# Memory's norm taken from the transposed copy of memory, and the first transfers cut in halves, in a two-layer decoder trunk

## The chip, the cores and the metric

The kernel runs on one core of one Trainium2 chip. The metric is the device time of the core in microseconds (us); a smaller number is better. Engines: TensorE (PE; its weight loads are listed as PEld), VectorE (DVE), ScalarE (ACT), GpSimd (POOL) and SyncE (SP), whose queue issues most of the DMA transfers.

## What is computed

A trunk of two layers over x (512 x 1024) with a memory of 256 rows of 1024. Each layer normalises x, projects it, runs 12 heads of forgetting attention (layer 0) or retention (layer 1) and 4 heads of attention over the memory, gates the result and projects it back:

```python
def reference(x, mem, norm_g, ...):
    mem_n = rmsnorm(mem, mem_norm_g)
    for i in range(DEPTH):
        h = rmsnorm(x, norm_g[i])
        ...
        memo = mem_cross_attention(q_mem, mem_n, w_mem_kv[i])
        o = jnp.concatenate([main, memo], axis=-1) * jax.nn.silu(z)
        x = x + o @ w_out[i]
    return rmsnorm(x, final_norm_g)

def rmsnorm(x, g):
    y = xf * lax.rsqrt(jnp.mean(xf * xf, axis=-1, keepdims=True) + EPS)
    return (y * g.astype(jnp.float32)).astype(x.dtype)

def mem_cross_attention(q_mem, mem_n, w_kv):
    kv = mem_n @ w_kv
    km, vm = split_cols(kv, [MEM_W, MEM_W])
    ...
```

The change is about `mem_n @ w_kv`. The kernel multiplies the unnormalised memory (times the gains) with the weights and applies the reciprocal root mean square of each memory row afterwards.

## The kernel before, in words

All weights come from DRAM in pieces of 128 x 1024 fp32 (512 KB). `load_piece` (L110) issues the transfer of the next piece of a fixed list on SP's queue into one of four buffers `raw`. `prep_piece` (L122) splits it in two rounded parts: a cast to `wH` on ScalarE (L136) and the remainder `wL = raw - wH` on VectorE (L137), each in one of four buffers; it then issues the next load. A piece is split when an earlier one is retired by TensorE. Only the first piece's cast is shared by VectorE (L131) and ScalarE (L132). Each product is computed as three: high x high, high x low, low x high.

The program starts with memory. `start_mem` (L743) issues, on SP's queue, the transposed memory in two halves of 512 KB (`vv<-in_memT_dram`; each holds four of the eight slices of 128 columns), four weight pieces, a small table, and then memory's 256 rows as they are, two transfers of 512 KB. The gains `gc` are a small transfer on ScalarE's queue. Then `emit` (L896) fills a warm-up tile with zeros on VectorE (L900) and runs 13 products of it on TensorE (L904). `first_splits` and `mem_split` split memory's slices, times the gains, in two parts (tiles `gg`; L768 and L160 on ScalarE, L769 and L161 on VectorE).

Real work begins with the values of layer 1 (`f_vm(1, ...)`): four pieces, in each two slices of memory against 512 columns, for two blocks of 128 memory rows: 12 products of 512 columns a piece, 48 in all, into two accumulators. The first piece's products stand with all `wH` first (L437), the others' mixed (L450). Four key heads follow (`f_km(1, h)`), 24 products of 256 columns each (L60). Then layer 0's keys and values of memory and the rest.

`memr_gen` (L774) makes the reciprocal roots: two squares over memory's rows with a running sum on ScalarE (L175), two small steps on GpSimd (L176, L177) for each of the two. The result `mr` scales the values as they leave PSUM, and `spread` (L180) turns it into a row over all partitions, `rbm`, by two products with the unit matrix (L183) and a copy (L185); the keys are multiplied by `rbm` (L417).

TensorE's order is the order in which the program is written (`MANUAL`). While the first four pieces are split, VectorE, ScalarE and GpSimd are also in written order. Elsewhere a scheduler places their instructions by priorities (`due`), and so the order on these engines shows in the built program only. SP is in written order up to the first layer.

Of the kernel before, what the change touches and what calls it, by code (L numbers as in the profile page):

```python
# [16 lines left out]
D = 1024  # L17
# [18 lines left out]
@with_exitstack  # L36
def tile_hybrid(ctx, tc, x_in, mem_in, memT_in, g_cols, norm_g, fin_g, b_f, wv0, wp, index, consts, cosT, sinT, dec, out):
    nc = tc.nc
# [41 lines left out]
    rbm = cst.tile([P, NMEM], F32, name="rbm")  # L80
    ident = csb[:, 0:P]
    nhalf = cst.tile([P, 1], F32, name="nhalf")
    G.memset(nhalf, -0.5)
# [84 lines left out]
    def acc_tile():  # L168
        return ps_at("acc", [P, 512], F32, name="acc")
# [233 lines left out]
    def f_km(l, h):  # L403
        key = (l, "km", h)

        def fn():
            H, L = pieces[key]
            mT = st["mT"]
            ps = acc_tile()
            terms = []  # L410
            for w, c in ((H, 0), (H, 1), (L, 0)):
                for k in range(KD):
                    terms.append((w[:, k * P:(k + 1) * P], mT[k][c]))
            mm_group(ps[:, :NMEM], terms)
            kt = tile_("km" if l == 0 else "qk", [P, 2, NMEM], F32R)
            kn = tile_("dd", [P, 512])
            V.tensor_tensor(out=kn[:, :NMEM], in0=ps[:, :NMEM], in1=rbm, op=ALU.mult)  # L417
            split_to(kt[:, 0, :], kt[:, 1, :], kn[:, :NMEM])
            st[l, "km", h] = kt
            retire(key)  # L420
        return [([key], fn)]

    def f_vm(l, plan, first=False):
        box = {}
        seen = {}

        def part(steps, final):
            mT = st["mT"]
            if first and steps[0][0] == 0:
                H, L = pieces[l, "vm", 0]  # L430
                for _, b in steps:
                    box[b] = acc_tile()
                for w, halves in ((H, (0, 1)), (L, (0,))):
                    for _, b in steps:
                        for k2 in range(2):
                            for c in halves:
                                PE.matmul(box[b], lhsT=mT[k2][c][:, b * P:(b + 1) * P], rhs=w[:, k2 * 512:(k2 + 1) * 512],  # L437
                                          start=(w is H and k2 == 0 and c == 0), stop=False)
                retire((l, "vm", 0))
                steps = []  # L440
            for i, b in steps:
                H, L = pieces[l, "vm", i]
                if b not in box:
                    box[b] = acc_tile()
                n = 0
                for k2 in range(2):
                    k = 2 * i + k2
                    for a, w in split3(mT[k][0][:, b * P:(b + 1) * P], mT[k][1][:, b * P:(b + 1) * P],
                                       H[:, k2 * 512:(k2 + 1) * 512], L[:, k2 * 512:(k2 + 1) * 512]):
                        PE.matmul(box[b], lhsT=a, rhs=w, start=(i == 0 and n == 0), stop=(i == 3 and n == 5))  # L450
                        n += 1
                seen[i] = seen.get(i, 0) + 1
                if seen[i] == 2:
                    retire((l, "vm", i))
            if final:
                if l == 1:
                    vm = [t[:, :1024].rearrange("p (b c) -> p b c", b=2) for t in pt_tiles()]
                else:
                    vm = [tile_("vv", [P, 2, 512], F32R) for _ in range(2)]
                for b in range(2):  # L460
                    split_to(vm[0][:, b, :], vm[1][:, b, :], box[b], st["mr"][b])
                st[l, "vm"] = vm
# [214 lines left out]
    def g_forget():  # L677
# [45 lines left out]
        norm=(0, 2),  # L723
        memr=(0, 2.4),
        xload=(0, 1, 2, 3, 4),
# [17 lines left out]
    def start_mem():  # L743
        nc.scalar.dma_start(out=gc, in_=g_cols)
        src = [tile_("vv", [P, 4, NMEM]) for _ in range(2)]
        rows = [tile_("vv", [P, D]) for _ in range(2)]
        nc.sync.dma_start(out=src[0], in_=memT_in[0])
        load_piece()
        nc.sync.dma_start(out=src[1], in_=memT_in[1])
        for _ in range(BUFS["raw"] - 1):  # L750
            load_piece()
        nc.sync.dma_start(out=csb, in_=consts[:, 0:P])
        for b in range(2):
            nc.sync.dma_start(out=rows[b], in_=mem_in[b * P:(b + 1) * P, :])
        st["msrc"], st["mrows"] = src, rows
# [29 lines left out]
    def build_layer(l):  # L785
# [13 lines left out]
        for pr in range(6):  # L799
# [28 lines left out]
    cycle(f_vm(1, [[(i, 0), (i, 1)] for i in range(4)], first=True) +  # L828
          sum([f_km(1, h) for h in range(4)], []), [("memr", (), 1.5), ("xload", (), 0.5)], mode=8)
    cycle(sum([f_km(0, h) for h in range(4)], []) + f_vm(0, [[(i, 0), (i, 1)] for i in range(4)]),  # L830
# [64 lines left out]
    def emit():  # L895
# [18 lines left out]
        for ci, (fillers, jobs, start, mode, last) in enumerate(cycles):  # L914
            if start == ("lead", 0):
                spill()
                lead.close()
                tro = tile_("dd", [P, 2 * P])
                tc.keep_in_program_order(nc.sync.dma_start(out=tro, in_=consts[:, P:3 * P]))
                tc.keep_in_program_order(A.copy(out=tri, in_=tro[:, :P]))  # L920
                tc.keep_in_program_order(A.copy(out=ones, in_=tro[:, P:]))
                nc.sync.dma_start(out=bfb, in_=b_f.partition_broadcast(P))
# [43 lines left out]
    tri = cst.tile([P, P], F32R, name="tri")  # L966
    ones = cst.tile([P, P], F32R, name="ones")
    bfb = cst.tile([P, 12], F32, name="bfb")
# [100 lines left out]
```

## Time and profile before

| what | value |
|---|---|
| median of 3 runs | 925.57 us (925.4 to 925.78) |
| the profiled execution | 925.52 us, its span 923.7 us |
| TensorE busy | 914.7 us of the span |
| VectorE, ScalarE, GpSimd busy | 593.5, 437.2, 33.6 us |
| DMA moved | 100.69 MB |

The span runs from the first to the last instruction. A row of the timeline gives the start, the busy time, the engine, the line, the operation and its tiles; in brackets stands how long the engine had been idle before, and what ended that. A busy engine is not an engine that could do no more: VectorE and ScalarE have room, and their idle time costs nothing while TensorE has its next operands in time.

### The profile page before, as it was taken

Reading aid. Unit: us, or ns where it says so; the run is one execution under the profiler, and the core shown is the slowest. Engines: PE = TensorE matmul, PEld = TensorE weight load, DVE = VectorE, ACT = ScalarE, POOL = GpSimd, SP = SyncE. Lnnn points to the kernel's source line nnn. Section 1 sums busy time; section 2 is a strip of 40 time slices with the busy share of each in tenths; the row PEclk is TensorE's granted clock in tenths of the full one; section 3 lists DMA queues with packets and bytes.
Section 4 is the critical chain, followed back from the end, with each engine's and each line's share of the span. In section 5 each row is a group of like instructions: output and inputs, shape, how many; then the busy total and the mean of one; then the engine's idle time right before and its main releaser. Section 6 shows DMA issues by size and latency. Waiting matters only on the chain.

```text
span 923.7 us, 12322 instructions
## 1 busy us (share of the span) xinstructions
PE 914.7 (99%) x4623; PEld 778.0 (84%) x4623; DVE 593.5 (64%) x1060; ACT 437.2 (47%) x767; POOL 33.6 (4%) x91
## 2 busy tenths in 40 slices
PE   9999999999999999999999999999999999999997
PEld 7998888888888888888898898888888888888985
DVE  6866664553755564645557756576678675888865
ACT  6744453332544233433325444454457464676642
POOL 0100100000000000000000010000000000000001
PEclk9999999999999999999999999999999999999999
DMA  9774322222332221423223152323323321632302
GB/s 337 265 258 142 116 92 92 90 71 69 127 101 81 78 94 53 144 78 103 81 95 100 46 160 70 109 73 95 111 87 119 114 81 58 182 103 81 115 1 91
DMA packets 32195, 100.69 MB, mean 109 GB/s; under 512 B 4348, under 2 KB 4860, under 8 KB 32136
## 3 DMA queue, kind: packets, MB, share of 16 engines
q1 hardware_dynamic: 30984, 97.55, 32.5%
q0 software_dynamic: 864, 2.10, 0.8%
q8 instruction: 36, 0.59, 0.3%
q10 hardware_dynamic: 288, 0.27, 0.1%
q14 instruction: 23, 0.19, 0.1%
HBM read 92.53 MB, written 4.22 MB: 105 GB/s over the span
## 4 chain that ended last, share of the span: by engine, by line
PE 98%; DMA 1%; issue 0%; DVE 0%; ACT 0%; SPq 0%; POOLq 0%; DVEq 0%; POOL 0%; ACTq 0%
PE acc L226 45%; PE acc L60 23%; PE acc L322 10%; PE s L60 6%; PE o L560 5%; PE acc L379 2%; PE acc L450 2%; PE pt L594 1%; PE o L60 1%; PE acc L385 1%; PE pt L529 1%; PE pt L202 1%; DMA raw<-in_wp_dram 1%; DVE wL L137 0%; ACT wH L136 0%
## 5 line engine op out<-in xcount | busy, mean ns | idle before, releaser
L137 DVE TENSOR_TENSOR wL<-raw,wH 128x1024 fp32r<-128x1024 f32 x148 | 180.8, 1224 | 103.9 <-ACT wH L136 64.0
L136 ACT CAST wH<-raw 128x1024 fp32r<-128x1024 f32 (+1 forms) x147 | 153.5, 1049 | 69.8 <-PE acc L226 34.8
L226 PE MATMUL acc<-hL,wH 128*128 128x512 f32 x608 | 163.6, 394 | 0.0
L226 PE MATMUL acc<-hH,wH 128*128 128x512 f32 x608 | 153.5, 394 | 0.0
L226 PE MATMUL acc<-hH,wL 128*128 128x512 f32 x608 | 150.6, 390 | 0.0
L60 PE MATMUL acc<-wH,gg 128*128 128x512 f32 x416 | 135.8, 393 | 0.0
L226 PEld LDWEIGHTS acc<-hH,wL 128*128 128x128 f32 x608 | 114.1, 188 | 24.5
L226 PEld LDWEIGHTS acc<-hH,wH 128*128 128x128 f32 x608 | 111.0, 188 | 21.3
L226 PEld LDWEIGHTS acc<-hL,wH 128*128 128x128 f32 x608 | 111.3, 188 | 20.6
L60 PEld LDWEIGHTS acc<-wH,gg 128*128 128x128 f32 x416 | 78.1, 188 | 15.6
L60 PE MATMUL acc<-wL,gg 128*128 128x512 f32 x208 | 81.1, 390 | 0.0
L342 DVE TENSOR_TENSOR x<-acc,x 128x512 f32<-128x512 f32 (+1 forms) x73 | 49.7, 681 | 38.2 <-PE acc L60 31.1
L157 ACT CAST pTH<-pt 128x128 fp32r<-128x128 f32 (+2 forms) x64 | 29.8, 467 | 63.2 <-PE pt L594 50.6
L584 ACT ACTIVATE p<-dd,nm 128x128 f32<-128x128 f32 (+3 forms) x48 | 27.0, 563 | 68.0 <-DVE nm L580 67.8
L60 PE MATMUL s<-qk 128*128 128x256 f32 (+3 forms) x240 | 53.5, 326 | 0.0
L322 PE MATMUL acc<-wH,hH 128*128 128x512 f32 x128 | 50.4, 394 | 0.0
L322 PE MATMUL acc<-wH,hL 128*128 128x512 f32 x128 | 49.9, 390 | 0.0
L158 DVE TENSOR_TENSOR pTL<-pt,pTH 128x128 fp32r<-128x128 f32 (+2 forms) x64 | 34.2, 536 | 24.3 <-ACT pTH L157 24.1
L322 PE MATMUL acc<-wL,hH 128*128 128x512 f32 x128 | 49.9, 390 | 0.0
L560 PE MATMUL o<-pTH,vv 128*128 128x512 f32 (+1 forms) x192 | 48.4, 314 | 0.0
L157 ACT CAST gg<-sz 128x512 fp32r<-128x512 f32 x28 | 17.4, 622 | 60.9 <-DVE sz L495 39.9
L60 PEld LDWEIGHTS s<-qk 128*128 128x128 f32 x240 | 40.3, 189 | 6.4 <-DVE p L634 0.3
(197 smaller groups left out, 1354.9 us busy)
## 6 DMA issues: line engine op xcount, KB each, us to landing
raw<-in_wp_dram SPq DMA_DIRECT2D x146, 512.0 KB, 3.6
cbc<-c_d SPq DMA_DIRECT2D x12, 256.0 KB, 3.4
cbc<-in_dec_dram SPq DMA_DIRECT2D x12, 256.0 KB, 3.2
dd<-dd SPq DMA_DIRECT2D x48, 64.0 KB, 2.0
x<-in_x_dram SPq DMA_DIRECT2D x4, 512.0 KB, 6.3
out_dram<-vv SPq DMA_DIRECT2D x3, 512.0 KB, 2.6
raw<-in_wv_dram SPq DMA_DIRECT2D x2, 536.0 KB, 4.2
vv<-in_memT_dram SPq DMA_DIRECT2D x2, 512.0 KB, 4.6
```

Of the source, the lines that this page charges most:

```text
L60: PE.matmul(ps, lhsT=l, rhs=r, start=(i == 0), stop=(i == n - 1))
L136: A.copy(out=H[:, :n], in_=raw[:, :n])
L137: V.tensor_tensor(out=L[:, :n], in0=raw[:, :n], in1=H[:, :n].bitcast(F32), op=ALU.subtract)
L157: A.copy(out=dH, in_=src)
L158: V.tensor_tensor(out=dL, in0=src, in1=dH.bitcast(F32), op=ALU.subtract)
L226: PE.matmul(box["ps"], lhsT=a[:, k * P:(k + 1) * P], rhs=b[:, k, :], start=(n == 0), stop=(n == 23))
L322: PE.matmul(ps, lhsT=a, rhs=b, start=(k == 0 and n == 0), stop=(k == KD - 1 and n == 2))
L342: V.tensor_tensor(out=dst, in0=ps, in1=dst, op=ALU.add)
L379: PE.matmul(ps, lhsT=a, rhs=b, start=(i == 0), stop=False)
L450: PE.matmul(box[b], lhsT=a, rhs=w, start=(i == 0 and n == 0), stop=(i == 3 and n == 5))
L560: PE.matmul(o[:, j * P:], lhsT=a, rhs=b, start=(j == 0 and i == 0), stop=(j == NT - 1 and i == 2))
L584: A.activation(p[:, :n], dd[:, :n], AF.Exp, bias=nm, scale=-1.0, accum_out=sm)
```

## The change

1. Memory's rows are not loaded any more. The sums of squares come from the transposed memory: two squares of 128 x 1024 on ScalarE, three additions on GpSimd that fold eight slices to one (128 x 256), a split in two parts, and four products of 16 columns against a matrix of ones, which sum over the partitions. Two roots on GpSimd follow.
2. The matrix of ones is loaded and rounded at the start, not before layer 0.
3. The first half of the transposed memory and the first weight piece are loaded in two transfers each, and the second piece's transfer stands ahead of memory's second half.
4. The second piece's products run with all `wH` first, as the first's; the values' two accumulators are of the kind `s`.
5. The values' scaling and the first key head's scaling are put off (`vmfin`, `kmfin`) until the roots and `rbm` are there; the first key head's products come ahead of the broadcast.

The core of the diff:

```diff
@@ load_piece
+            elif i == 0:
+                for c in (0, 512):
+                    nc.sync.dma_start(out=raw[:, c:c + 512], in_=wp[index[key], :, c:c + 512])
@@ f_km
+            retire(key)
+            def finish():
+                kt = tile_("km" if l == 0 else "qk", [P, 2, NMEM], F32R)
+                kn = tile_("dd", [P, 512])
+                V.tensor_tensor(out=kn[:, :NMEM], in0=ps[:, :NMEM], in1=rbm, op=ALU.mult)
+                split_to(kt[:, 0, :], kt[:, 1, :], kn[:, :NMEM])
+                st[l, "km", h] = kt
+            if (l, h) == (1, 0):
+                st["kmfin"] = finish
+            else:
+                finish()
@@ f_vm, part
-            if first and steps[0][0] == 0:
+            if first and steps[0][0] < 2:
...
-                    for _, b in steps:
-                        for k2 in range(2):
+                    for k2 in range(2):
+                        for _, b in steps:
                             for c in halves:
...
-        memr=(0, 2.4),
+        memr=(0, 2.6, 3.6),
@@ start_mem
-        rows = [tile_("vv", [P, D]) for _ in range(2)]
-        nc.sync.dma_start(out=src[0], in_=memT_in[0])
+        nc.sync.dma_start(out=src[0][:, :2, :], in_=memT_in[0, :, :2, :])
+        load_piece()
+        nc.sync.dma_start(out=src[0][:, 2:, :], in_=memT_in[0, :, 2:, :])
         load_piece()
         nc.sync.dma_start(out=src[1], in_=memT_in[1])
-        for _ in range(BUFS["raw"] - 1):
+        nc.sync.dma_start(out=csb, in_=consts[:, 0:P])
+        st["ones"] = tile_("dd", [P, P])
+        nc.sync.dma_start(out=st["ones"], in_=consts[:, 2 * P:3 * P])
+        for _ in range(BUFS["raw"] - 2):
             load_piece()
-        nc.sync.dma_start(out=csb, in_=consts[:, 0:P])
-        for b in range(2):
-            nc.sync.dma_start(out=rows[b], in_=mem_in[b * P:(b + 1) * P, :])
@@ memr_gen
-        st["mr"] = [rstd_of(st["mrows"][b], st["mrows"][b], f"mr{b}") for b in range(2)]
+        A.copy(out=ones, in_=st["ones"])
+        sq = [tile_("vv", [P, 4, NMEM]) for _ in range(2)]
+        for i in range(2):
+            A.activation(sq[i], st["msrc"][i], AF.Square)
+        G.tensor_tensor(out=sq[0], in0=sq[0], in1=sq[1], op=ALU.add)
+        G.tensor_tensor(out=sq[0][:, :2, :], in0=sq[0][:, :2, :], in1=sq[0][:, 2:, :], op=ALU.add)
+        G.tensor_tensor(out=sq[0][:, 0, :], in0=sq[0][:, 0, :], in1=sq[0][:, 1, :], op=ALU.add)
+        sh = tile_("dd", [P, 2, NMEM], F32R)
+        split_to(sh[:, 0, :], sh[:, 1, :], sq[0][:, 0, :])
+        yield
+        pb = ps_at("t", [P, 2, 16], F32, name="pt")
...
+        for b in range(2):
+            mm_group(pb[:, b, :], [(sh[:, c, b * P:(b + 1) * P], ones[:, :16]) for c in range(2)])
+        A.copy(out=ss2, in_=pb[:, :, 0:1])
+        for b in range(2):
...
+            G.tensor_scalar(out=r, in0=ss2[:, b, :], scalar1=1.0 / D, scalar2=EPS, op0=ALU.mult, op1=ALU.add)
+            G.tensor_tensor(out=r2, in0=r, in1=nhalf, op=ALU.pow)
+            st["mr"].append(r2)
+        st["vmfin"]()
         yield
         spread(st["mr"], rbm)
+        st["kmfin"]()
         yield
```

How it moves the instructions is seen in the built program. First VectorE, from its first row on; before:

```order
L900 MEMSET dd 128x512
L131 CAST wH<-raw 128x512
L769 SCALAR_TENSOR_TENSOR gg<-vv,gc,gg 128x256 x2
L137 TENSOR_TENSOR wL<-raw,wH 128x1024
L161 SCALAR_TENSOR_TENSOR gg<-vv,gc,gg 128x256 x2
L137 TENSOR_TENSOR wL<-raw,wH 128x1024
```

and with the change:

```order
L135 CAST wH<-raw 128x512
L787 SCALAR_TENSOR_TENSOR gg<-vv,gc,gg 128x256 x2
L141 TENSOR_TENSOR wL<-raw,wH 128x1024
L165 SCALAR_TENSOR_TENSOR gg<-vv,gc,gg 128x256 x2
L940 MEMSET dd 128x512
L141 TENSOR_TENSOR wL<-raw,wH 128x1024
```

The MEMSET of the warm-up tile (`dd`), the first row before, now stands sixth to seventh, behind the first piece's rows and four splits of memory, though its lines of the source are as they were.

TensorE's first rows, with the engines that they wait for in brackets; before:

```order
L904 MATMUL acc<-dd 128x512 [waits DVE_49]
L904 MATMUL acc<-dd 128x512 x12
L437 MATMUL acc<-wH,gg 128x512 [waits DVE_49,Activation_49]
L437 MATMUL acc<-wH,gg 128x512 [waits DVE_49]
L437 MATMUL acc<-wH,gg 128x512 [waits Activation_49]
...
L437 MATMUL acc<-wL,gg 128x512 [waits DVE_49]
L437 MATMUL acc<-wL,gg 128x512 x3
```

and with the change:

```order
L944 MATMUL acc<-dd 128x512 [waits DVE_49]
L944 MATMUL acc<-dd 128x512 x12
L449 MATMUL s<-wH,gg 128x512 [waits Activation_49]
L449 MATMUL s<-wH,gg 128x512 x3
L449 MATMUL s<-wH,gg 128x512 [waits Activation_49]
L449 MATMUL s<-wH,gg 128x512 x3
L449 MATMUL s<-wL,gg 128x512 x4
```

The order of the products is the same here; the waits for VectorE behind the warm-up are gone, and the warm-up's own has stayed.

Then ScalarE, from the fourth piece's cast (the first row of each) to the broadcast's copy (`rbm`); before:

```order
L136 CAST wH<-raw 128x1024 [waits DMAHW6_49]
L175 ACTIVATE vv,ss<-vv 128x1024 [waits DMAHW0_49]
L175 ACTIVATE vv,ss<-vv 128x1024 [waits DMAHW1_49]
L136 CAST wH<-raw 128x1024 [waits DMAHW2_49,DVE_49,PE_49]
L160 ACTIVATE pTH<-acc,mr_232 128x512 [waits PE_49,Pool_49]
L136 CAST wH<-raw 128x1024 [waits DMAHW3_49,DVE_49]
L185 COPY rbm<-pt 128x256 [waits PE_49]
```

and with the change:

```order
L140 CAST wH<-raw 128x1024 [waits DMAHW2_49]
L140 CAST wH<-raw 128x1024 [waits DMAHW3_49,DVE_49,PE_49]
L140 CAST wH<-raw 128x1024 [waits DMAHW4_49,DVE_49,PE_49]
L795 ACTIVATE vv<-vv 128x1024 x2
L140 CAST wH<-raw 128x1024 [waits DMAHW5_49,DVE_49,PE_49]
L161 CAST dd<-vv 128x256 [waits Pool_49]
L140 CAST wH<-raw 128x1024 [waits DMAHW6_49,DVE_49,PE_49]
L807 COPY ss_281<-pt 128x2 [waits PE_49]
L164 ACTIVATE pTH<-s,mr_288 128x512 [waits Pool_49]
L164 ACTIVATE pTH<-s,mr_292 128x512 [waits Pool_49]
L140 CAST wH<-raw 128x1024 [waits DMAHW0_49,DVE_49,PE_49]
L196 ACTIVATE vv,ss<-x_83 128x1024 [waits DMAHW3_49]
```

The two squares (L175, now L795) stood right behind the fourth piece; now the casts of the fifth and sixth piece, which wait for TensorE, stand ahead of them, and GpSimd's result is waited for by a cast between two further pieces. The copy of `rbm` comes behind the rows shown.

## Rows read from the trace of the kernel before

**Rows 1.** Page: busy us by engine; TensorE's granted clock; one group (busy us, mean ns).

```profile
PE 914.7 (99%) x4623; PEld 778.0 (84%) x4623; DVE 593.5 (64%) x1060; ACT 437.2 (47%) x767; POOL 33.6 (4%) x91
...
PEclk9999999999999999999999999999999999999999
...
L226 PE MATMUL acc<-hH,wL 128*128 128x512 f32 x608 | 150.6, 390 | 0.0
```

**Rows 2.** View of waits, TensorE, whole span: us in total, times, longest us.

```profile
PE acc L904 <- DVE dd L900: 1.4, 1, 1.4
PE acc L450 <- DVE wL L137: 0.8, 1, 0.8
```

**Rows 3.** Timeline, TensorE and its weight loads, to 19 us: start us, us, then names.

```profile
1.44 5.42 PE L904 MATMUL acc<-dd 128*128 128x512 f32 x13 [1.44 <-DVE dd L900]
...
6.47 1.79 PEld L437 LDWEIGHTS acc<-wH,gg 128*128 128x128 f32 x8
...
9.52 0.19 PEld L450 LDWEIGHTS acc<-wH,gg 128*128 128x128 f32 x1 [0.35 <-ACT wH L136]
...
10.78 0.19 PEld L450 LDWEIGHTS acc<-wL,gg 128*128 128x128 f32 x1 [1.07 <-DVE wL L137]
...
10.89 0.42 PEld L450 LDWEIGHTS acc<-wH,gg 128*128 128x128 f32 x2
...
18.63 0.64 PEld L183 LDWEIGHTS pt<-csb,mr 128*128 128x128 f32 x4
...
19.18 1.98 PEld L60 LDWEIGHTS acc<-gg,wH 128*128 128x128 f32 x16
```

**Rows 4.** Timeline, VectorE and ScalarE up to the fourth piece.

```profile
0.90 0.48 DVE L900 MEMSET dd<- 128x512 f32 x1 [0.90 <-PEq L1057]
...
4.76 0.91 ACT L768 ACTIVATE gg<-vv,gc 128x256 fp32r<-128x256 f32 x2 [2.09 <-DMA gc<-in_gcols_dram]
5.84 0.62 ACT L132 CAST wH<-raw 128x512 fp32r<-128x512 f32 x1 [0.17 <-DMA raw<-in_wp_dram]
5.84 0.43 DVE L131 CAST wH<-raw 128x512 fp32r<-128x512 f32 x1 [4.45 <-DMA raw<-in_wp_dram]
6.18 0.88 DVE L769 SCALAR_TENSOR_TENSOR gg<-vv,gc,gg 128x256 fp32r<-128x256 f32 x2
...
6.97 1.22 DVE L137 TENSOR_TENSOR wL<-raw,wH 128x1024 fp32r<-128x1024 f32 x1
8.11 0.88 DVE L161 SCALAR_TENSOR_TENSOR gg<-vv,gc,gg 128x256 fp32r<-128x256 f32 x2
...
8.43 1.05 ACT L136 CAST wH<-raw 128x1024 fp32r<-128x1024 f32 x1 [1.16 <-DMA raw<-in_wp_dram]
...
9.38 0.90 ACT L160 ACTIVATE gg<-vv,gc 128x256 fp32r<-128x256 f32 x2
...
13.37 1.22 DVE L137 TENSOR_TENSOR wL<-raw,wH 128x1024 fp32r<-128x1024 f32 x1
```

**Rows 5.** Windows: busy us (count) by engine, granted clock, DMA share, GB/s.

```profile
6.00:9.00 3.00, 3.00 (x15) 2.46 (x14) 2.98 (x6) 1.84 (x4) 0.00 (x0) 1.00 1.03 422
```

**Rows 6.** Timeline: memory's squares and roots; split of a 128x256 tile.

```profile
12.87 1.06 ACT L175 ACTIVATE vv<-vv 128x1024 f32<-128x1024 f32 x1
...
15.35 0.19 POOL L176 TENSOR_SCALAR rstd<-ss 128x1 f32<-128x1 f32 x1
...
15.63 0.56 POOL L177 TENSOR_TENSOR mr<-rstd,nhalf 128x1 f32<-128x1 f32 x1
...
23.02 0.41 ACT L157 CAST qk<-dd 128x256 fp32r<-128x256 f32 x1 [0.68 <-DVE dd L417]
...
24.04 0.42 DVE L158 TENSOR_TENSOR qk<-dd,qk 128x256 fp32r<-128x256 f32 x1
```

**Rows 7.** Groups of GpSimd by shape, whole span: busy us, mean ns, idle before.

```profile
L575 POOL TENSOR_SCALAR_AFFINE_SELECT dd<-dd 128x128 f32<-128x128 f32 x48 | 16.3, 341 | 369.5 <-DVE dd L574 369.5
...
L872 POOL TENSOR_TENSOR rstdf<-ss,rstdf 128x1 f32<-128x1 f32 x3 | 0.6, 192 | 5.7 <-ACT dd L868 5.7
```

More of the change, by code (lines that the diff above doesn't have):

```diff
@@ L81, in tile_hybrid @@
     ident = csb[:, 0:P]
+    ones = cst.tile([P, P], F32R, name="ones")
     nhalf = cst.tile([P, 1], F32, name="nhalf")
@@ L428, in part @@
             mT = st["mT"]
-            if first and steps[0][0] == 0:
-                H, L = pieces[l, "vm", 0]
-                for _, b in steps:
-                    box[b] = acc_tile()
+            if first and steps[0][0] < 2:
+                i = steps[0][0]
+                H, L = pieces[l, "vm", i]
+                if i == 0:
+                    for _, b in steps:
+                        box[b] = ps_at("s", [P, 512], F32, name="s")
                 for w, halves in ((H, (0, 1)), (L, (0,))):
-                    for _, b in steps:
-                        for k2 in range(2):
+                    for k2 in range(2):
+                        for _, b in steps:
                             for c in halves:
-                                PE.matmul(box[b], lhsT=mT[k2][c][:, b * P:(b + 1) * P], rhs=w[:, k2 * 512:(k2 + 1) * 512],
-                                          start=(w is H and k2 == 0 and c == 0), stop=False)
-                retire((l, "vm", 0))
+                                PE.matmul(box[b], lhsT=mT[2 * i + k2][c][:, b * P:(b + 1) * P], rhs=w[:, k2 * 512:(k2 + 1) * 512],
+                                          start=(i == 0 and w is H and k2 == 0 and c == 0), stop=False)
+                retire((l, "vm", i))
                 steps = []
@@ L455, in part, with finish @@
             if final:
-                if l == 1:
-                    vm = [t[:, :1024].rearrange("p (b c) -> p b c", b=2) for t in pt_tiles()]
-                else:
-                    vm = [tile_("vv", [P, 2, 512], F32R) for _ in range(2)]
-                for b in range(2):
-                    split_to(vm[0][:, b, :], vm[1][:, b, :], box[b], st["mr"][b])
-                st[l, "vm"] = vm
+                def finish():
+                    if l == 1:
+                        vm = [t[:, :1024].rearrange("p (b c) -> p b c", b=2) for t in pt_tiles()]
+                    else:
+                        vm = [tile_("vv", [P, 2, 512], F32R) for _ in range(2)]
+                    for b in range(2):
+                        split_to(vm[0][:, b, :], vm[1][:, b, :], box[b], st["mr"][b])
+                    st[l, "vm"] = vm
+                if first:
+                    st["vmfin"] = finish
+                else:
+                    finish()
         res, used = [], set()
@@ L828, in tile_hybrid @@
     cycle(f_vm(1, [[(i, 0), (i, 1)] for i in range(4)], first=True) +
-          sum([f_km(1, h) for h in range(4)], []), [("memr", (), 1.5), ("xload", (), 0.5)], mode=8)
+          sum([f_km(1, h) for h in range(4)], []), [("memr", (), 1.2), ("xload", (), 0.5)], mode=8)
     cycle(sum([f_km(0, h) for h in range(4)], []) + f_vm(0, [[(i, 0), (i, 1)] for i in range(4)]),
@@ L917, in emit @@
                 lead.close()
[L918 to L921, printed above, removed]
+                tro = tile_("dd", [P, P])
+                tc.keep_in_program_order(nc.sync.dma_start(out=tro, in_=consts[:, P:2 * P]))
+                tc.keep_in_program_order(A.copy(out=tri, in_=tro))
                 nc.sync.dma_start(out=bfb, in_=b_f.partition_broadcast(P))
```

21 lines of the change are left out of this document (9 added, 12 removed).

## Prediction

> **What bounds the kernel now.** I read the page's head first: TensorE is busy 914.7 of 923.7 us and its clock is at the upper level in all slices [rows 1]. So time can go or come only where TensorE stands idle. The view of its waits lists all of them: 1.4 us before the warm-up products, and 0.8 us for one rounding remainder [rows 2]. The timeline of the opening shows both in place [rows 3]: the 13 warm-up products of line 904 start at 1.44, the first real weight load at 6.47; then the loads stand still for 0.35 us until a cast on ScalarE is done and for 1.07 us until VectorE has a remainder. From 10.89 on, load follows load to the end of the program. Whatever shifts that dense stretch shifts the end by as much, and the change can win no more than those two holes.
>
> The pace: from the load at 10.89 to the one of line 183 at 18.63 there are 34 products of 512 columns, 0.2276 us each; the 48 of memory's values then need 10.92 us without a hole, and took 18.63 - 6.47 = 12.16 [rows 3]. The warm-up ones took 5.42 us for 13, 0.42 each: that is the clock's lower level, 1.2 GHz, left at the end of the warm-up.
>
> **What the change moves.** The important move is not in the diff. The scheduler places the MEMSET of the warm-up tile on VectorE, and nothing in the change keeps it in front: before, it is VectorE's first row; now it stands behind the first piece's cast, two splits of memory, the piece's remainder and two further splits (the first pair of fences above). All of these need transfers. TensorE's first row, the warm-up, waits for that MEMSET, and every real product is queued behind the 13 warm-up ones. The waits confirm it: the first real products no longer wait for VectorE, since the MEMSET's own signal already covers the remainder before it.
>
> **Late start, +7.3 us.** VectorE's present rows are the cast at 5.84, splits from 6.18, remainder 6.97 to 8.19, splits 8.11 to 8.99 [rows 4]. With the same arrivals the MEMSET (0.48 us) would run from about 8.9 to 9.4, and the warm-up start 0.06 later at 9.44 instead of 1.44: 8.0 us, the upper end. The halved transfers help: 422 GB/s [rows 5] move 512 KB in 1.24 us, so the second half of the first weight piece, with 256 KB less ahead of it, lands about 0.6 us earlier, near 5.2 instead of 5.8. ScalarE still has its two splits first (4.76 to 5.67), then casts at 5.58 instead of 5.84, to 6.20. VectorE's two splits no longer follow its cast at 5.84 but run by 6.2, so the remainder starts at 6.28 instead of 6.97, and what follows moves by 0.7: 7.3. If the vector of gains and the first half of memory also land 0.6 earlier, ScalarE starts sooner and it is 6.7, the lower end. I take 7.3, since ScalarE's first wait is put down to the small transfer of the gains, which is not halved [rows 4]. The 13 warm-up products then cost what they cost now; had all run at the lower level (0.427 each) it would be some 0.5 more.
>
> **Holes closed, -1.24 us.** With so late a start both roundings of the first four pieces are done before TensorE asks (the fourth's remainder ended at 14.6 even with an early start [rows 4]; the first real product would now come at 6.47 + 7.3 = 13.8 and need the fourth piece at 22). So the products-first order and the halved transfers win the whole 12.16 - 10.92, but no more, and they win it whatever the order within the second piece.
>
> **Four small products, +0.5 us.** The reductions against ones have 16 columns but load 128 x 128 weights; the loads of line 60 come at 0.12 us each (16 in 1.98 [rows 3]); four are 0.5.
>
> **A new wait on the sums of squares, +2.2 us.** Call the first real product 0. Before, the squares read rows of their own and their result was ready at 16.2, before TensorE asked at 18.63 [rows 3, 6]. Now ScalarE has, ahead of the two squares, the casts of pieces five and six, and the sixth may only overwrite the rounded weights of the second once their last use, the 20th product, is through: 19 x 0.2276 + 0.39 for its own length [rows 1] + 0.08 to take the signal = 4.8. ScalarE's rows of 128x1024 follow at 0.96 each (8.43 to 9.38 [rows 4]) and last 1.06 [rows 6], so the second square ends at 4.8 + 2 x 0.96 + 1.06 = 7.78. GpSimd then adds in three steps, 1024 + 512 + 256 = 1792 columns, call it X; then a cast (0.41) and a remainder (0.42) of 128x256 [rows 6] with three hand-overs of 0.07: 1.05. TensorE is through with its 48 products at 10.92 and waits 7.87 + X + 1.05 - 10.92 = X - 2.0. No row shows X. GpSimd's select of 128x128 takes 0.341, its one-column add 0.192 [rows 7]: (0.341 - 0.192)/127 = 1.17 ns a column for one operand. By that X = 3 x 0.19 + 2.10 + 0.16 between them = 2.8; with two operands read one after the other, 4.9. The wait is thus 0.8 to 2.9. I take X = 4.2 and 2.2 us, nearer the upper end because each add reads two tiles. The Trainium skill (GPSIMD Engine Reference, Elementwise, side-by-side cycle accounting) gives 4497 ns for a two-operand add of 2048 fp32 columns; an estimate by that rate is 3.9 for the 1792, and with it the sum would be 0.3 lower.
>
> **At nothing.** The two 512 KB loads of rows that go were behind the first pieces in the queue, and no TensorE wait there is for a transfer [rows 2]. The squares keep their size, 1.06 each [rows 6]. The four GpSimd steps to the reciprocal roots (0.19 and 0.55 us [rows 6]; with the copy out of PSUM about 2.3) lie beside the first key head, 24 products at 0.12 = 2.9, which was put in front of the broadcast: 0.6 spare. That head's finish comes late: ScalarE has two value splits, a cast and a square of x before it copies the broadcast, and VectorE the normalisation of x. The fourth key head needs that accumulator 2.9 + 0.5 + 5.8 = 9.2 after the small products; by the same durations it comes free at about 8.5. If this cover goes, the fourth head is late. Past this point the orders differ little and TensorE sets the pace; the loads, issued by VectorE's progress, are ahead of it by the 7 us.
>
> **Sum.** 7.3 - 1.24 + 0.5 + 2.2 = 8.8. The profiled execution took 925.52 (span 923.7); its median of runs is 925.57, so nothing is to be corrected. 925.5 + 8.8 = **934.3 us**.
>
> **Rivals.**
> *GpSimd's sums are hidden.* X under 2.0 leaves no wait: 932.1. Against it is the 1.17 ns a column; for it, that I price an add by a select. Chance 0.08.
> *VectorE stretches GpSimd's adds, or the fourth head is late.* A remainder of 1.22 us [rows 4] on VectorE falls into the adds (the seventh piece's, 9.5 to 10.7 on the count above); if it holds them off for its length, the end is 935.5. About as much if the fourth head's 0.6 spare fails. The Trainium skill (GPSIMD Engine Reference, Specifications) says GpSimd's SBUF interfaces are shared with VectorE and contended by VectorE instructions with two SBUF inputs, which the remainder is; no row here shows the two together. Chance 0.14.
> *The clock falls in the new wait.* It is low after the idle start [rows 3], and the hole of 1.07 us did not lower it; one of 2.2 or more might. Coming back took 4.6 us at the start; key products of 256 columns at 1.2 GHz need 0.213 instead of 0.12, so 4.6 us lose 2.0: 936.3. The Trainium skill (TensorE: Matmul & The Clock Gate, Part 1: The HAM clock gate) says that an idle TensorE falls back to the half rate; the trace agrees for the start only. Chance 0.13.
> *The warm-up is not held.* If the MEMSET still ran at 0.9, products would start at 6.47, and with the sums of squares also hidden the result is 925.5 - 1.24 + 0.5 = 924.8, not slower. This decides once late start and new wait together are under 2.6. Against it: the order is VectorE's program, and an engine runs its instructions in order; and with an early start the sixth piece's load, which waits for the second piece's remainder, would itself make the squares late. Chance 0.03.
>
> **How the numbers follow.** The forecast has 0.60; 0.02 is left for something unseen. A difference under 0.2%, 1.85 us, is about what a measurement of this kernel cannot tell from no change. The forecast's own ends are 925.5 + 6.7 - 1.24 + 0.5 + 0.8 = 932.3 and 925.5 + 8.0 - 1.24 + 0.5 + 2.9 = 935.7. The range takes in part of the hidden sums below and the clock's fall above: 931.8 to 937.0. All cases but the last rival and half of the unseen one are slower: slower 0.96, same 0.03, faster 0.01.
>
> **What would show it.** In the changed profile the MEMSET of the warm-up tile stands at about 8.2 us on VectorE, the warm-up starts at 8.7, the first product of s at 13.8; the 48 run without a hole; then one wait of about 2 us before the products with ones, put down to VectorE's remainder, with three GpSimd adds of 4.2 us together ahead of it. I am wrong if the warm-up starts before 5 us, if a hole of over 1 us stands elsewhere, or if the three adds take under 2 or over 5.5 us.

## The result, and the profile after

The changed kernel took **939.48 us** (median of 4 runs: 935.9, 939.52, 939.58, 939.44) against 925.67 before (4 runs, 925.4 to 926.32): a ratio of 1.0139, 95% interval 1.0114 to 1.0163. It is slower, as forecast, but the median lies 2.5 us above the top of the range. The profiled execution is the one of 935.9 (span 934.1), whose TensorE had a mean granted clock of 0.999; the three others had 0.994 and spans of 937.6 to 937.8. So the profile shows 10.4 of the 13.8 us; where the rest is was a question for the experiments.

The page after, beside [rows 1]: busy us by engine, TensorE by slices, and its clock.

```profile
PE 915.0 (98%) x4627; PEld 778.6 (83%) x4627; DVE 594.8 (64%) x1061; ACT 438.1 (47%) x767; POOL 39.4 (4%) x94
...
PE   5899999999999999999999999999999999999997
...
PEclk9999999999999999999999999999999999999999
```

TensorE is busy for as long as before; the span is 10.4 us longer and its first slices are emptier. The clock reads 9 or more in all slices; its records begin only where it first rises, at 13.81 us here and at 6.14 before, and ahead of that the views show 1.00 although the warm-up products come 0.43 us apart, behind it 0.23. So neither a page nor a mean clock tells how late the first rise is. TensorE's waits, beside [rows 2] (us in total, times, longest us):

```profile
PE acc L944 <- DVE dd L940: 9.6, 1, 9.6
PE pt L60 <- ACT dd L161: 2.6, 1, 2.6
PE pt L60 <- DVE dd L162: 0.2, 1, 0.2
```

The wait for the MEMSET has grown from 1.4 to 9.6, the wait of 0.8 inside the values is gone, and there is a new one of 2.6 for a cast of the sums. Now the timeline of the opening. First VectorE and ScalarE up to the warm-up, beside [rows 4]:

```profile
3.85 0.91 ACT L786 ACTIVATE gg<-vv,gc 128x256 fp32r<-128x256 f32 x2 [1.19 <-DMA gc<-in_gcols_dram]
...
5.98 0.62 ACT L136 CAST wH<-raw 128x512 fp32r<-128x512 f32 x1 [1.22 <-DMA raw<-in_wp_dram]
...
7.53 0.91 ACT L164 ACTIVATE gg<-vv,gc 128x256 fp32r<-128x256 f32 x2 [0.94 <-DMA vv<-in_memT_dram]
...
9.01 0.48 DVE L940 MEMSET dd<- 128x512 f32 x1
...
9.55 5.21 PE L944 MATMUL acc<-dd 128*128 128x512 f32 x13 [9.55 <-DVE dd L940]
```

The MEMSET stands behind the rows that the built order named and runs at 9.01 instead of 0.90; the warm-up starts 0.54 later. Memory's first quarter comes early (split at 3.85, before 4.76), but the second half of the first weight piece is cast at 5.98, later than the whole piece before (5.84), and memory's second quarter is split only at 7.53. The DMA windows of the two kernels beside each other tell why (us; busy us and count of PE, PEld, DVE, ACT, POOL; granted clock, DMA share, GB/s). Before:

```profile
4.00:6.00 2.00, 2.00 (x6) 1.52 (x6) 0.16 (x1) 1.07 (x3) 0.00 (x0) 1.00 1.02 412
```

After:

```profile
4.00:6.00 2.00, 0.00 (x0) 0.00 (x0) 1.22 (x3) 0.78 (x3) 0.00 (x0) 1.00 0.94 239
```

With the first transfers in halves, the DMA engines are still shown as busy (0.94) but move 239 GB/s where whole pieces moved 412. Then the values, the sums and the products with ones:

```profile
14.37 1.80 PEld L449 LDWEIGHTS s<-wH,gg 128*128 128x128 f32 x8
...
20.30 2.00 ACT L795 ACTIVATE vv<-vv 128x1024 f32<-128x1024 f32 x2
...
22.39 2.40 POOL L796 TENSOR_TENSOR vv<-vv 128x1024 f32<-128x1024 f32 x1 [21.54 <-ACT vv L795]
...
24.06 1.81 DVE L141 TENSOR_TENSOR wL<-raw,wH 128x1024 fp32r<-128x1024 f32 x1 [2.40 <-ACT wH L140]
...
24.87 2.12 POOL L797 TENSOR_TENSOR vv<-vv 128x512 f32<-128x512 f32 x1
...
25.27 0.39 PE L462 MATMUL s<-wH,gg 128*128 128x512 f32 x1
...
27.07 0.72 POOL L798 TENSOR_TENSOR vv<-vv 128x256 f32<-128x256 f32 x1
...
28.28 0.19 PEld L60 LDWEIGHTS pt<-ones,dd 128*128 128x128 f32 x1 [3.05 <-ACT dd L161]
...
28.74 0.41 PEld L60 LDWEIGHTS pt<-ones,dd 128*128 128x128 f32 x3 [0.27 <-DVE dd L162]
...
29.07 1.98 PEld L60 LDWEIGHTS acc<-gg,wH 128*128 128x128 f32 x16
```

The first real load is at 14.37; the last of the values' 48 products starts at 25.27, so they ran without a hole. GpSimd starts its adds at 22.39, when TensorE has 2.9 us of work left, and needs 5.40 us. TensorE's loads stand still for 3.05 us, then 0.27 more for the remainder, and the first key head begins at 29.07. By the first load for layer 0's projections of x (line 60, `wH,hH`) the program is 10.3 us late, 66.98 instead of 56.66; the end is late by 10.4. So all of it lies in the opening.

### The profile page after: what moved, and what is told of

It is laid out like the page before. It is cut to its first block, busy times and chain, and to the rows that moved or that the text cites. A ratio compares the mean times of both kernels' runs of the same rounds, so it can differ in the third digit from the quotient of the medians.

```text
span 934.1 us, 12332 instructions
## 1 busy us (share of the span) xinstructions
PE 915.0 (98%) x4627; PEld 778.6 (83%) x4627; DVE 594.8 (64%) x1061; ACT 438.1 (47%) x767; POOL 39.4 (4%) x94
## 4 chain that ended last, share of the span: by engine, by line
PE 97%; POOL 1%; DMA 1%; issue 0%; ACT 0%; DVE 0%; SPq 0%; POOLq 0%; DVEq 0%; ACTq 0%
PE acc L230 45%; PE acc L60 23%; PE acc L326 9%; PE s L60 6%; PE o L577 5%; PE acc L383 2%; PE pt L611 1%; PE acc L462 1%; PE o L60 1%; PE acc L389 1%; PE pt L546 1%; PE pt L206 1%; DMA vv<-in_memT_dram 1%; PE acc L944 1%; PE s L449 0%
```

## Experiments

All comparisons are with the kernel before on the same chip (medians 925.5 to 925.7). Theory A: the late warm-up comes from the order in the ring of `dd` tiles alone; the wait is GpSimd's adds; the 3.6 us between 935.9 and 939.5, which the profile does not show, are the clock, which falls in or behind that wait. Against it: the halves or the new sums push the MEMSET back as well; the 3.6 us are late transfers, which no filling of the wait would bring back.

**again: the changed kernel once more** (no edit, one execution).

> The changed kernel once more, for a second profile. Its four runs so far were 935.9 (the profiled one, mean granted clock 0.999) and 939.4 to 939.6 (0.994). Theory A (the clock falls to its lower level in the 3.05 us in which TensorE waits for the sums of squares): a run of about 939.5 shows the same waits to within 0.2 us, and a stretch of half clock that begins between 25 and 33 us and lasts about 7 us, with the key heads' products inside it. Rival B (the clock rises later at the start): the stretch of half clock reaches into the values' products, before 25 us, and the products of s start later than 14.4.

Measured: 937.0 us, mean clock 0.996. The waits were the same (9.7, 2.6, 0.2), but the clock was not:

```profile
30.00:32.00 2.00, 2.00 (x12) 2.00 (x11) 0.30 (x2) 0.95 (x2) 1.38 (x4) 0.50 0.48 145
...
34.00:40.00 6.00, 6.00 (x53) 6.00 (x52) 4.90 (x7) 4.83 (x11) 3.29 (x6) 1.00 0.57 215
```

The granted clock, the figure after the five busy times, is 0.50 (1.2 GHz) from 30 to 32 and back at 1.00 from 34; by its records it is low from 29.94 to 33.35. TensorE had waited until 27.92, and the products that ran in the low stretch are the first key head's:

```profile
27.92 0.28 PE L60 MATMUL pt<-ones,dd 128*128 128x16 f32 x1 [2.62 <-ACT dd L161]
...
28.74 2.81 PE L60 MATMUL acc<-gg,wH 128*128 128x256 f32 x16
...
33.05 0.75 PE L187 MATMUL pt<-csb,mr 128*128 128x128 f32 x4
```

From 28.74 to 33.05 the 24 products took 4.31 us; in the profile of 935.9 they took 2.95 (29.10 to 32.05). That is a loss of 1.4 us, and it comes in an execution whose wait was no longer than that one's. Theory A holds for what it says of the place; the stretch was half as long as it expected, and the execution was not one of 939.5.

**look2, look3: two more profiles of the changed kernel**, to catch an execution like the three of 939.5.

> The changed kernel, a second further look, to catch one of the executions of 939.5 in a profile. Theory (the 3.6 us that the profile of 935.9 does not show are a longer low stretch of the clock that begins in or behind the new wait): if it takes 939 to 940, the granted clock is 0.5 for some 7 to 9 us from about 28 to 30 us on, the key heads' products take about twice their time in it, and the waits are those of the first profile. Rival (late transfers or another wait): the clock is at 1.0 throughout, and a wait of over 2 us stands somewhere that the first profile does not have. At 935 to 937 it tells neither.

> As the look before it, a third one: the same numbers are expected of it by both theories.

Measured: 939.78 and 938.91 us, both at the mean clock of 0.994 that those three had. The waits are those of the first profile (9.5 and 9.0 for the MEMSET; 3.05 us for the sums in both). In look2, by windows and by TensorE's loads:

```profile
31.00:33.00 2.00, 2.00 (x12) 2.00 (x11) 0.30 (x2) 0.74 (x2) 1.59 (x4) 0.50 0.40 88
...
37.00:39.00 2.00, 2.00 (x19) 2.00 (x18) 1.28 (x3) 1.50 (x3) 1.67 (x3) 1.00 0.50 100
```

```profile
29.13 0.19 PEld L60 LDWEIGHTS pt<-ones,dd 128*128 128x128 f32 x1 [3.05 <-ACT dd L161]
...
30.18 3.53 PEld L60 LDWEIGHTS acc<-gg,wH 128*128 128x128 f32 x16
...
35.30 0.92 PEld L187 LDWEIGHTS pt<-csb,mr 128*128 128x128 f32 x4
36.14 1.98 PEld L60 LDWEIGHTS acc<-gg,wH 128*128 128x128 f32 x16
```

The clock is at 0.50 in all of 31 to 35 and back at 1.00 from 37; by the records of the clock itself it is low from 29.30 to 36.12, in look3 from 28.44 to 35.27: 6.8 us, twice the 3.4 us of `again`. From the first product with ones to the second key head TensorE took 36.14 - 29.13 = 7.01 us (6.95 in look3), where the profile of 935.9 has 32.39 - 28.28 = 4.11. So the fall costs 2.8 to 2.9 us, and 1.5 in `again` by the same count (33.53 - 27.92 = 5.61). For look3 that is 2.84 of its difference of 3.0; its wait ends 0.14 later. look2 has 0.85 more ahead of the wait, where its clock rose only at 15.64, after the first real products had begun (14.82); in the profile of 935.9 it rose at 13.81, before them. No further wait of over 0.2 us is to be seen, so late transfers are out.

**ones_dd: the ones in the ring, and nothing else** (the kernel before, with one more early tile).

```diff
@@ start_mem, behind the load of csb
+        st["ones"] = tile_("dd", [P, P])
+        nc.sync.dma_start(out=st["ones"], in_=consts[:, 2 * P:3 * P])
@@ memr_gen, first line
+        A.copy(out=ones, in_=st["ones"])
@@ emit, start of layer 0
-                tro = tile_("dd", [P, 2 * P])
+                tro = tile_("dd", [P, P])
```

> The kernel before, with one part of the change alone: the matrix of ones is loaded at the start into a buffer of the ring dd, ahead of the warm-up tile, which is of the same ring. Transfers are whole, memory's rows are loaded and squared as before. Theory A (the ring holds the MEMSET back): the MEMSET stands behind the first pieces on VectorE at about 8.9 us, the warm-up starts 8 us late, the two holes of 1.24 us close, and there is no wait for roots: 925.5 + 8.0 - 1.2 = 932.3, with no spread over runs. Rival B (the late start comes of the halved transfers or of the new rows on VectorE): no change, 925.5.

Measured: 934.81 us (934.0 to 934.94), ratio 1.0098 [1.0083, 1.0113]. TensorE has one wait, and VectorE shows its cause:

```profile
PE acc L908 <- DVE dd L904: 11.5, 1, 11.5
```

```profile
9.68 1.23 DVE L138 TENSOR_TENSOR wL<-raw,wH 128x1024 fp32r<-128x1024 f32 x1 [0.49 <-ACT wH L137]
10.96 0.48 DVE L904 MEMSET dd<- 128x512 f32 x1
```

The warm-up starts 11.50 - 1.44 = 10.06 us late and the first real load 16.80 - 6.47 = 10.33. The two holes of the values are hidden behind it, but the clock rises only at 17.14, so the values take 11.09 us (16.80 to 27.89) instead of 12.16, and not 10.92. The sum, 925.7 + 10.33 - 1.07 = 935.0, meets the 934.94 of the profiled execution. I had expected 932.3, with the MEMSET one place further forward. Four lines about a matrix of ones cost 9 us: neither the halves nor the new sums are needed for it. The warm-up tile is now taken from the ring `dd` after a tile whose transfer stands late in SP's written order, and the built program has the MEMSET further back. The next run shows that it is the shared ring that does it; the ring has five buffers, so it is not short of them, and why the scheduler picks just this place no run shows.

**own: the ones in a tile of their own** (the changed kernel otherwise).

```diff
-        st["ones"] = tile_("dd", [P, P])
+        st["ones"] = cst.tile([P, P], F32, name="onesf")
```

> The changed kernel with the matrix of ones loaded into a tile of its own instead of the ring dd; nothing else is changed. Theory A: the MEMSET is VectorE's first row again and real products start at 6.5; but then the wait on the sums of squares grows, since the two squares stand behind casts that wait for TensorE and GpSimd's three adds need 5.2 us: the values end near 19 (late halves cost about 1.7), the sums come near 29, so 936 without and 939.5 with a fall of the clock. Rival B (the ring is the whole loss beside the wait of the profile): 8.1 us come back, 928 to 931.5.

Measured: 939.67 us (938.99 to 940.4), ratio 1.0152 [1.0137, 1.0167]; mean clocks 0.990 to 0.992. The warm-up starts at 1.44 again and the first real load is at 5.74, and all that it won is lost:

```profile
PEld pt L60 <- ACT dd L161: 9.4, 1, 9.4
PEld s L449 <- ACT wH L140: 2.2, 1, 2.2
PEld acc L944 <- DVE dd L940: 1.4, 1, 1.4
```

```profile
L796 POOL TENSOR_TENSOR vv<-vv 128x1024 f32<-128x1024 f32 x1 | 2.3, 2337 | 23.9 <-ACT vv L795 23.9
L797 POOL TENSOR_TENSOR vv<-vv 128x512 f32<-128x512 f32 x1 | 1.3, 1262 | 0.1
L798 POOL TENSOR_TENSOR vv<-vv 128x256 f32<-128x256 f32 x1 | 0.7, 722 | 0.1
```

```profile
22.67 2.00 ACT L795 ACTIVATE vv<-vv 128x1024 f32<-128x1024 f32 x2
```

With an early start the pieces' casts wait for transfers, the squares come behind the cast of the eighth piece (their row starts at 22.67), and TensorE waits 9.4 us for the sums. The clock is at its lower level around that wait (25.03 to 35.27), and another time behind the hole of 2.2 us, which ended at 10.65 (11.38 to 14.79). So the late warm-up hid most of a second fault of the change: the place of the squares. The adds also show GpSimd by itself, with VectorE idle beside it: 2.34, 1.26 and 0.72 us (the figure after the comma is the mean in ns).

**fill: TensorE kept at work in the wait** (the changed kernel, with 12 products into an accumulator that nobody reads).

```diff
@@ memr_gen, ahead of the products with ones
+        for i in range(12):
+            PE.matmul(idle, lhsT=m0[:, :P], rhs=m0, start=(i == 0), stop=(i == 11))
```

> The changed kernel with 12 products of 512 columns that nothing reads, put on TensorE between the values and the products with ones, where it waits 3 us; at 0.227 each they need 2.7 us. The output is the reference's. Theory A (the 3.6 us between the runs of the changed kernel are a fall of the clock in that wait): all runs lie together, near 935.9 (up to 1 more, as the copy of the sums now stands behind a square of x on ScalarE), with a mean clock of 0.999. Rival B (the clock's late rise at the start, or something later): runs of 939 to 941 with 0.994 stay.

Measured: 936.5 us (935.4, 936.77, 936.87, 936.23), ratio 1.0119 [1.0102, 1.0136]; mean clocks 0.998 to 0.999. In the profile these products fill 24.80 to 27.68, and the first product with ones starts at 27.63. Nothing is done sooner in this kernel, the sums come when they come; but no execution reaches 939, and no mean clock of the four is below 0.998, where six of the changed kernel's seven had 0.996 or less. So it is the idleness in the wait that the fall follows on.

**sums: the squares right behind the first four pieces, the adds on VectorE** (the changed kernel, its late warm-up kept).

```diff
-    def memr_gen():
+    def sums():
...
-        G.tensor_tensor(out=sq[0], in0=sq[0], in1=sq[1], op=ALU.add)
+        V.tensor_tensor(out=sq[0], in0=sq[0], in1=sq[1], op=ALU.add)
```

(The diff is shortened. The two further adds likewise; `sums` is called in `emit` behind the four pieces, in written order.)

> The changed kernel with the sums of squares made earlier: the two squares right behind the first four pieces on ScalarE, the three adds on VectorE instead of GpSimd, both in written order. The late warm-up stays. Theory A (late start plus a wait of 2.8 us plus the clock's fall in it): the wait before the products with ones is gone, no run shows a fall of the clock, and all runs lie together at 925.6 + 8.1 (start) - 1.2 (holes) + 0.5 (small products) = 933.0, up to 1 more or less with the start. Rival B (the clock falls for another cause): runs of over 936 stay.

Measured: 933.4 us (932.94 to 934.01), ratio 1.0084 [1.0071, 1.0098], clocks 0.998 to 0.999. There is no wait ahead of the products with ones any more:

```profile
16.56 1.23 DVE L796 TENSOR_TENSOR vv<-vv 128x1024 f32<-128x1024 f32 x1 [0.69 <-ACT vv L795]
...
19.08 0.69 DVE L797 TENSOR_TENSOR vv<-vv 128x512 f32<-128x512 f32 x1
...
21.79 0.42 DVE L798 TENSOR_TENSOR vv<-vv 128x256 f32<-128x256 f32 x1
...
25.49 0.64 PEld L60 LDWEIGHTS pt<-ones,dd 128*128 128x128 f32 x4
```

VectorE does in 2.34 us what took GpSimd 5.24, and it is done before TensorE asks. What remains is the late start (first real load at 14.57) and 0.5 us of waits for the roots at the broadcast. This run moves the squares and the adds together and does not tell which of the two was needed.

**own_sums: both repairs** (`sums`, with the ones in a tile of their own, and the broadcast behind the second key head, so that two heads' scaling is put off). The halves stay.

> As sums, and the matrix of ones in a tile of its own, and the products with ones behind the first key head, the broadcast behind the second (their two finishes put off). The halved first transfers stay. Theory A: start at 6.0 to 6.5 and no wait on the sums; what is left beside the 0.5 of the small products is the late arrival of the halves, which kept TensorE waiting 1.8 to 2.2 us for the second piece's cast with a fall of the clock in that hole: 927 to 928.5. Rival C (halving the first transfers costs nothing): 924.9.

Measured: 928.07 us (927.66 to 928.96, 7 runs), ratio 1.0028 [1.0018, 1.0039]. The waits that are left are those of late operands (the casts and remainders of the second and third piece) and of the roots:

```profile
PEld pt L187 <- POOL mr L813: 1.9, 2, 1.6
...
PEld s L462 <- DVE wL L141: 1.1, 1, 1.1
PEld s L449 <- ACT wH L140: 0.9, 1, 0.9
```

```profile
4.00:6.00 2.00, 2.00 (x8) 1.55 (x8) 1.22 (x3) 0.91 (x3) 0.00 (x0) 1.00 0.99 289
```

**best: both repairs and whole transfers** (`own_sums` otherwise).

```diff
-        nc.sync.dma_start(out=src[0][:, :2, :], in_=memT_in[0, :, :2, :])
+        nc.sync.dma_start(out=src[0], in_=memT_in[0])
         load_piece()
-        nc.sync.dma_start(out=src[0][:, 2:, :], in_=memT_in[0, :, 2:, :])
         load_piece()
         nc.sync.dma_start(out=src[1], in_=memT_in[1])
```

(In `load_piece` the two half transfers are one again.)

> As own_sums, with the first half of memory and the first piece in one transfer each as before the change, the second piece still ahead of memory's second half. Theory A: no hole in the values, no wait on the sums: 925.6 - 1.2 + 0.5 = 924.9, 0.1% under the kernel before, just clear of its spread. Rival: a wait for the accumulators of the first key heads, whose finishes come late: up to 926.5.

Measured: 926.24 us (925.98 to 928.22, 11 runs), ratio 1.0010 [1.0001, 1.0019]. Against `own_sums` the halves alone cost 1.8 us; from 4 to 6 us that one moved 289 GB/s, this one 410. The values now end at 17.58, before at 18.63 [rows 3]: 1.05 won. More than that is given back: the products with ones take 0.74 (from 20.55 to 21.29) with a wait of 0.22 in them, the waits in the key heads are 0.24, 0.23 and 0.16, and layer 0's first load for x stands at 57.13 instead of 56.66.

```profile
4.00:6.00 2.00, 2.00 (x6) 1.52 (x6) 0.27 (x1) 1.18 (x3) 0.00 (x0) 1.00 1.01 410
```

```profile
17.58 2.09 PEld L60 LDWEIGHTS acc<-gg,wH 128*128 128x128 f32 x16
...
20.96 0.41 PEld L60 LDWEIGHTS pt<-ones,dd 128*128 128x128 f32 x3 [0.22 <-DVE dd L159]
21.29 1.98 PEld L60 LDWEIGHTS acc<-gg,wH 128*128 128x128 f32 x16
...
24.48 0.30 PEld L184 LDWEIGHTS pt<-csb,mr 128*128 128x128 f32 x2 [0.24 <-POOL mr L809]
```

So the change, repaired wherever the runs had shown a fault, comes out within 0.2% of the kernel before.

**best2: one GpSimd step for both blocks** (`best`, with one scaling step instead of two).

> As the version before (best), with one GpSimd step instead of two for the scaled sums of both blocks. Theory (0.47 us of waits at the broadcast come from two first steps of GpSimd that take 1.43 together): the wait goes, 925.7. Rival (the key heads behind are late anyway): 926.2.

Measured: 926.11 us (925.69 to 927.08, 11 runs), ratio 1.0007 [0.9998, 1.0016]. The profile (925.79 us) has no wait for the roots left, but the single step took 1.41 us where the two had taken 1.43: its price does not lie in the number of steps. The wait went because the step began 0.43 us earlier (21.94 against 22.37): ScalarE's copy of the sums stands behind a piece's cast, whose transfer was there earlier (the cast at 20.75 against 21.17). By the medians, 0.13 apart, the two versions cannot be told apart.

**reorder: the kernel before, with the order of the change and what goes with it.** By the runs so far, what had won 1.05 us was the order of the first transfers and products. Here memory's rows, their squares and the warm-up tile are left as they were before.

```diff
@@ start_mem
         load_piece()
+        load_piece()
         nc.sync.dma_start(out=src[1], in_=memT_in[1])
-        for _ in range(BUFS["raw"] - 1):
+        for _ in range(BUFS["raw"] - 2):
             load_piece()
@@ f_vm, part
-            if first and steps[0][0] == 0:
+            if first and steps[0][0] < 2:
@@ emit, behind the four pieces, in written order
+            st["mr"] = [rstd_of(st["mrows"][b], st["mrows"][b], f"mr{b}") for b in range(2)]
```

(The values' accumulators are of kind `s`, their scaling is put off behind the broadcast as in the change, and VectorE, ScalarE and GpSimd follow the written order through the key heads.)

> The kernel before, with its memory rows, its squares behind the first four pieces and its warm-up tile untouched; taken from the change are only the second piece's load ahead of memory's second half (whole transfers), the second piece's products with the rounded weights first, the accumulators of kind s and the values' scaling put off behind the broadcast. Theory (the part of the change worth having is the order of the first transfers and products; all else in it costs): the two holes of 0.35 and 1.07 us go, the warm-up stays at 1.44, nothing new is waited for, and the opening is 1.0 to 1.2 us shorter: 924.3 to 924.6. Rival (what the values win is given back at the broadcast or the key heads, as in the version before this one): 925.3 to 926.

Measured: **924.05 us** (923.91 to 924.58, 11 runs) against 925.51 (21 runs), ratio 0.9986 [0.9977, 0.9995].

```profile
PE acc L912 <- DVE dd L908: 1.4, 1, 1.4
```

```profile
6.52 1.78 PEld L439 LDWEIGHTS s<-wH,gg 128*128 128x128 f32 x8
...
17.41 0.64 PEld L183 LDWEIGHTS pt<-csb,mr 128*128 128x128 f32 x4
```

The only wait left is that for the warm-up tile. The broadcast's loads come at 17.41 instead of 18.63 [rows 3]; layer 0's first load for x stands at 55.45 instead of 56.66, so all of the 1.2 us gets through. This is the version that beats both. The gain of 0.14% is less than the 0.2% named in the prediction, and only the many runs tell it from nothing. How it is shared among the order, the accumulators and the put-off scaling was not tried.

## Why the prediction was wrong

By its own steps, against the profile of 935.9 us:

| step | forecast, us | measured, us |
|---|---|---|
| late start, first real load | +7.3 (6.7 to 8.0) | +7.90 (14.37 - 6.47) |
| holes closed | -1.24 | -1.25 (values 10.91 instead of 12.16: their last load, at 25.05, and 0.23 for it end at 25.28) |
| new wait on the sums | +2.2 (0.8 to 2.9) | +3.00 (28.28 - 25.28) |
| four small products | +0.5 | +0.79, with 0.27 of wait for the remainder |
| elsewhere | 0 | -0.06 |
| sum | +8.8 | +10.4 |

**What held.** The move that the diff does not show was the main one, and the ring experiment put 9 us on it alone. The holes went for the amount forecast, whatever the products' order. The wait stands where it was said to, ahead of the products with ones, though it is put down to ScalarE's cast of the sums (3.05) and for only 0.27 to VectorE's remainder, which the forecast had named. The second square ended 7.93 us after the first real load, 7.78 forecast. The two loads of rows that went, and the fourth key head, cost and gave nothing: neither shows in the list of waits.

**The late start was mis-sized by 0.6.** The step was "422 GB/s [rows 5] move 512 KB in 1.24 us, so the second half of the first weight piece, with 256 KB less ahead of it, lands about 0.6 us earlier". Halves moved 239 GB/s from 4 to 6 us; the half came later than the whole had, and memory's second quarter with it. The full +8.0, with no help from the halves, was the better term. `best` against `own_sums` confirms the sign: whole transfers are 1.8 us faster.

**The new wait was mis-sized by 0.8.** X was taken as 4.2 and measured 2.40 + 2.12 + 0.72 = 5.24, and 5.40 with the hand-overs between. By themselves (`own`) the three took 4.32, or 4.48 with the hand-overs, so X was 0.3 short as it stood. The other 0.9 is the rival "VectorE stretches GpSimd's adds", which had 0.14: the add of 512 columns ran beside VectorE's remainder and took 2.12 instead of 1.26, and that remainder 1.81 instead of 1.22 [rows 4]. All five profiles in which the two meet (this one, `again`, look2, look3, `fill`) have 2.12 to 2.15 and 1.81; no run moved the remainder alone. Of this 1.2, 0.56 came back, since the first product with ones waits for the cast alone (0.49 from the last add's end to it, 1.05 forecast with the remainder); 0.15 was added by the squares. The Trainium skill (GPSIMD Engine Reference, Specifications) says that VectorE instructions with two SBUF inputs contend with GpSimd for its SBUF interfaces; the two rows agree, and both engines are slower in them.

**The step that failed is the clock.** With the terms as measured but no fall the result would have been 925.5 + 10.4 = 935.9, inside the range, and one of four executions came out there. The rival "the clock falls in the new wait" had a chance of 0.13 and a price of 2.0. It happened in all three further profiles (937.0, 939.78, 938.91), and by the mean clocks in three of the first four executions; the profiled one of those four is the exception. It belonged in the sum, as a part of the wait. The price, worked out from a stretch of 4.6 us, was too low as well: its rate of 2.0 us for 4.6 was right, but the stretch was 6.8 us in the two profiles that are like the median, and cost 2.8 to 2.9. With that the forecast's own 934.3 would be 937.2, above the range, while the mis-sized terms alone stay inside it. Of the 3.6 us between 935.9 and the median the fall so explains 2.9. The rest can be a late first rise as in look2, where it cost up to 0.85; the three executions near the median have no profile, and it stays open. My reason against the fall was that "the hole of 1.07 us did not lower it"; a hole of 1.07 is no evidence on one three times as long, and in `own` a hole of 2.2 was followed by a fall. The Trainium skill (TensorE: Matmul & The Clock Gate, Part 1: The HAM clock gate) says that an idle TensorE falls back to the half rate; the further profiles agree, with 0.50 behind the wait, and the profile of 935.9 shows that the same wait can also pass without a fall. Which of the three an execution gets (no fall, 3.4 us or 6.8 us) stays open.

**The rival on the other side** (the warm-up not held, 924.8) was rightly doubted for both its reasons: the warm-up was held, and in `own`, where it was not, the squares came so late that the kernel took 939.67. They stood there behind the eighth piece's cast, two further back than the prediction had counted.

## What to carry to other kernels

- Before a tile is added near the start, see in the built order where the first instruction of TensorE's chain ends up: a buffer taken from a shared ring by an unrelated small tile can put the warm-up behind data that it does not need (here 9 us for four lines).
- Price a new wait of some us on TensorE twice, once for its length and once for the clock that can fall behind it; keep the two as one case, not as case and rival.
- When a change bundles several edits, run them apart: here the order of two loads and of one piece's products, with the accumulators and the put-off scaling that go with it, was worth 1.5 us, and the rest of the change cost 15.

## What was not expected of the hardware

- Two transfers of 256 KB in place of one of 512 KB: 239 GB/s from 4 to 6 us instead of 412, while the DMA engines are shown as busy for 0.94 of it (289 against 410 in `own_sums` and `best`, which differ in the halves alone).
- GpSimd's two-operand fp32 add of 512 columns: 1.26 us by itself, 2.12 beside a VectorE subtraction of 1024 columns, which itself took 1.81 instead of 1.22. By themselves the three adds of `own` (0.72, 1.26 and 2.34 us for 256, 512 and 1024 columns) lie on one line: 0.18 us and 2.10 ns a column, an estimate from these three.
- After a wait of 3.05 us the granted clock was 0.50 for a stretch that began at or behind the wait's end (0.0, 0.2 and 2.0 us after it), with TensorE at work again; it lasted 3.4 us in one execution and 6.8 in two, and in a fourth with the same wait the clock stayed at 1.00. With products that nobody reads in the wait (`fill`) no mean clock of four was below 0.998.
- GpSimd's scaling at the roots took 1.43 us for two steps of one column in `best` and 1.41 for one step of two columns in `best2`; two steps took 0.46 in `own`, and in the kernel before 0.52 and 0.19 (the second in [rows 6]). The cause was not tried.
